# Values, memory queries and three gate sets of layer 2 as seven block products each (Strassen), in a stage of their own with the memory attention

## The chip, the cores and the metric

The kernel runs on one core of a Trainium2 chip. The metric is the device time of one execution in microseconds (us), the median of several runs. Engines are named as in the profile: PE is TensorE (PEld its weight loads), DVE is VectorE, ACT ScalarE, POOL GpSimd, and SP the engine that issues every DMA of this kernel, in order, from one queue.

## The reference

One sequence of 2048 tokens with 1024 features runs through two layers. What matters here is layer 2:

```python
def dilated_mixer(h, w_in):
    for g, (window, dil) in enumerate(((128, 1), (512, 4), (2048, 16))):
        base = g * 3 * 768
        qkv = (h @ w_in[:, base:base + 3 * 768]).reshape(B, T, 3, 6, 128)
        q, k = partial_rope(qkv[:, :, 0], pos), partial_rope(qkv[:, :, 1], pos)
        o, lse = dilated_group(q, k, qkv[:, :, 2], window, dil)
        outs.append(o); lses.append(lse)
    wts = softmax(stack(lses), axis=0)
    o = einsum('gbth,gbthd->bthd', wts, stack(outs)).reshape(B, T, 768)
    q_mem, gate = split(h @ w_in[:, 6912:], [256], axis=-1)
    return o, q_mem, gate

for i in range(2):
    h = rmsnorm(x, norm_w[i])
    mix, q_mem, gate = gla_mixer(h, ...) if i == 0 else dilated_mixer(h, w_in_b[0])
    mem_o = memory_attention(q_mem, mem_n, w_memkv[i])
    x = x + (concatenate([mix, mem_o], -1) * silu(gate)) @ w_out[i]
return rmsnorm(x, final_norm_w)
```

The input projection of layer 2 has 8192 columns: for each of three groups g (window and dilation) 768 query, 768 key and 768 value columns (6 heads of 128), then from column 6912 on 256 memory queries, and from 7168 on 1024 gate columns. The last 256 gate columns (7936) belong to the memory attention, which has 4 heads of 64 over 256 memory tokens.

## The kernel before

Every projection is done with fp16 operands that are split into a high and a low part. `mm3` (lines 174 to 177) multiplies high by high, high by low and low by high into one fp32 accumulator, so each product of 128 features costs three matmuls, and a projection runs over eight such slices of the 1024 features (`KT` = 8).

**Layer 1** runs to about 914 us. Its last loop goes over 16 blocks of 128 tokens (`NB`): `a2_out` adds the block's output to x, `a2_h2` (from line 677) normalizes it for layer 2, transposes it on PE and writes it, split, into `h2T` ([128, 2, 8, 2048]: features on partitions; high and low part; slice of the features; token). h2T stays on chip for the whole of layer 2.

**Weights.** `load_w` (line 106) fetches 1024 x 256 columns of a matrix, sums the squares of all its elements on ACT, adds the 128 partitions' sums with a matmul against a matrix of ones (`ones`, fp32; line 124), scales the weights by the result and splits them: ACT makes the high part (line 134), DVE the low one (line 135). `load_w256` uses it for layer 2. Four weight buffers (`wpb`) rotate.

**Nine units** follow, one for each pair of heads hp (0 to 2) and each group g (0 to 2). Per unit `proj_v` (line 771) makes the values of both heads for 16 token blocks: 16 x 8 x 3 = 384 matmuls with h2T as the stationary operand and 256 weight columns moving. `proj_qk` (line 791) makes one head's queries and keys: 8 x 24 = 192 matmuls of 512 columns, the rotary step on DVE and POOL (line 809), and the split. `attend` (line 818) takes the 16 query blocks of a head in 8 steps of two: scores on PE, maximum, exponential, then `split_P` (line 165), which splits the probabilities (ACT, POOL at line 169) and transposes them by a DMA (line 170, tiles `ph` to `pt`), and the product with the values. A head's output is copied (line 874) and written to DRAM (`od`, line 875), as are the row maxima and sums (`std`, line 888). The program interleaves: the attention of a head is written around the projection of the next one, and the V projection of the next unit follows.

**Gates.** When all three groups of a head pair are done, `gate_prep` (line 893) reads the maxima and sums back (tiles `nm` and `dn`, line 898), works out the weights of the three groups and writes them to DRAM (`fd`). `gate_item` (line 928) treats one head and 512 tokens: `gate_mm` does 24 matmuls of 512 columns and the SiLU; a DMA broadcasts the weights to all partitions (`fb`, line 934), three more read the outputs of the groups (`og`, lines 937 to 939); POOL (lines 940, 945) and DVE (lines 942, 948, 949, 951) combine them; the result goes to DRAM (`brd`, line 952). The pool `gk` holds one fb and one og. Eight items make a head pair. Those of hp 0 stand in unit (1, 0), those of hp 1 in the last unit, those of hp 2 in the tail.

**The tail** (about 2337 to 2550 us) goes over 16 token blocks with the memory attention: `mem_q` (line 958) projects the queries of a block with 24 matmuls of 256 columns, `mem_scores` (line 236) transposes them on PE and makes scores, softmax and `split_P`, `mem_pv` (line 265) the product with the memory values, `mem_out` (line 967) the product with its gate. The items of hp 2 and the memory gate's tiles are placed between the blocks. Then comes the output projection (from line 1065), which reads `brd` back.

**What sets the order.** The program is written in the order above, but a scheduler that simulates the engines' times (`schedule_with_timeline_sim`, line 1165) reorders the instructions of each engine, within what buffers and data allow; each engine, and SP's queue, then runs its own list strictly in order. For matmul results there are two banks `ps_mm`, one `ps_x`, two `ps_tr`, two `ps_g` and one `ps_o`.

## Time and profile before

| | us |
|---|---|
| runs of the kernel before | 2711.78, 2716.41, 2717.67 |
| median | 2716.41 |
| profiled execution, its span | 2713.5 |
| busy PE, DVE, ACT, POOL | 2603.2, 1510.0, 1128.4, 496.9 |
| layer 1, to about | 914 |
| units up to the last one's second head | 914 to 2301 |
| last attention of the units | 2301 to 2337 |
| tail with the memory attention | 2337 to 2550 |
| output projection | 2550 to 2713 |

The profiled execution has no other time of its own than its span. The profile lists for each engine how long it was busy; matmuls overlap, so that a busy PE is not one at its peak, and the distance from one matmul's start to the next says more. The clock that PE was granted is given as a share of full speed. A row of the table by stage holds one stretch of the span; a row of grouped instructions holds the source line, engine, operation, tiles written and read, shape, count, busy time and mean duration, and the idle time before them with what ended it. Rows with three durations give lowest, middle and highest in ns, and the first and last start.

### The profile page before, as it was taken

To read this page: it belongs to the slowest core of one execution; us is meant where nothing else is said; L and a number is where in the kernel's file an instruction comes from. 1 tells how busy PE (TensorE), PEld (TensorE's weight loads), DVE (VectorE), ACT (ScalarE), POOL (GpSimd) and SP (SyncE) were. 2 spreads that over 40 slices of the span, in tenths; PEclk is the share of its full clock that TensorE was granted. 3 is DMA by queue.
4 is the path that set the end of the run, shared out by engine and by line. 5 is a ranking of instruction groups with operands and counts; after the bars stand their busy time and mean duration, and the time that the engine had idled before them with its cause. 6 is when DMAs were issued, how large, how long until landed. Compare 5 with 4: busy or idle time off the path is not lost. (4 is left out here: it accounts for less than half of the span.)

```text
span 2713.5 us, 47912 instructions
## 1 busy us (share of the span) xinstructions
PE 2603.2 (96%) x19166; PEld 1937.0 (71%) x19166; DVE 1510.0 (56%) x3349; ACT 1128.4 (42%) x2621; POOL 496.9 (18%) x421
## 2 busy tenths in 40 slices
PE   7999999999999999999999998999999999788999
PEld 6889998899988845858475474756667574455687
DVE  6445443665555466373746637465555637777433
ACT  6356444543434434252425324243433434535322
POOL 0000000010101023131313314222222313443000
PEclk9999999999999999999999999999999999899999
DMA  5242113333332213130313535122322224776543
GB/s 202 84 143 74 65 57 94 119 90 96 91 96 81 91 47 86 34 90 26 87 53 100 121 86 135 38 68 73 78 62 62 72 65 128 197 172 139 158 148 114
DMA packets 377539, 259.23 MB, mean 96 GB/s; under 512 B 250674, under 2 KB 340452, under 8 KB 377316
## 3 DMA queue, kind: packets, MB, share of 16 engines
q1 hardware_dynamic: 377316, 256.17, 33.7%
q8 instruction: 150, 2.46, 0.4%
q14 instruction: 73, 0.60, 0.1%
HBM read 149.63 MB, written 60.21 MB: 77 GB/s over the span
## 5 line engine op out<-in xcount | busy, mean ns | idle before, releaser
L175 PE MATMUL ps_mm<-w,hT 128*128 128x256 f16 (+1 forms) x1408 | 387.2, 275 | 3.7 <-DVE ws L128 1.8
L176 PE MATMUL ps_mm<-w,hT 128*128 128x256 f16 (+1 forms) x1408 | 385.9, 275 | 0.0
L177 PE MATMUL ps_mm<-w,hT 128*128 128x256 f16 (+1 forms) x1408 | 385.2, 275 | 0.4 <-DVE hT L370 0.4
L175 PE MATMUL ps_mm<-h2T,w 128*128 128x512 f16 x944 | 359.2, 380 | 0.5 <-DVE qm L232 0.4
L177 PE MATMUL ps_mm<-h2T,w 128*128 128x512 f16 x944 | 358.8, 380 | 0.6 <-DVE cols L306 0.6
L176 PE MATMUL ps_mm<-h2T,w 128*128 128x512 f16 x944 | 358.9, 380 | 0.0
L809 POOL TENSOR_TENSOR sh<-sh,rope 32x512 f32<-32x512 f32 x144 | 183.2, 1272 | 629.8 <-DVE sh L808 623.3
L177 PEld LDWEIGHTS <-w 128*128 128x128 f16 x1408 | 139.1, 99 | 148.1 <-issue 3.0
L175 PEld LDWEIGHTS <-w 128*128 128x128 f16 x1408 | 138.5, 98 | 144.5 <-issue 2.4
L176 PEld LDWEIGHTS <-w 128*128 128x128 f16 x1408 | 138.5, 98 | 144.0 <-issue 2.8
L175 PE MATMUL ps_mm<-w,h2T 128*128 128x256 f16 x840 | 229.2, 273 | 0.5 <-DVE sg L301 0.5
L176 PE MATMUL ps_mm<-w,h2T 128*128 128x256 f16 x840 | 229.5, 273 | 0.0
L177 PE MATMUL ps_mm<-w,h2T 128*128 128x256 f16 x840 | 229.4, 273 | 0.0
L854 ACT ACTIVATE pm<-pm,st,cols 128x256 f32<-128x256 f32 (+1 forms) x288 | 156.2, 543 | 135.7 <-DVE st L848 134.6
L169 POOL TENSOR_TENSOR ph<-pm,ph 128x512 f16<-128x512 f32 (+2 forms) x144 | 143.5, 1001 | 291.5 <-issue 158.8
L175 PE MATMUL ps_x<-h2T,w 128*128 128x512 f16 x464 | 177.4, 382 | 0.3 <-DVE v L787 0.3
L176 PE MATMUL ps_x<-h2T,w 128*128 128x512 f16 x464 | 177.2, 382 | 0.0
L177 PE MATMUL ps_x<-h2T,w 128*128 128x512 f16 x464 | 177.1, 382 | 0.0
L169 POOL TENSOR_TENSOR stg<-mp,stg 128x512 f16<-128x512 f32 x16 | 18.5, 1159 | 833.9 <-DMA ogd<-og 457.7
L176 PEld LDWEIGHTS <-h2T 128*128 128x128 f16 x1280 | 149.4, 117 | 10.1 <-issue 2.5
L175 PEld LDWEIGHTS <-h2T 128*128 128x128 f16 x1280 | 149.5, 117 | 7.7
L176 PEld LDWEIGHTS <-hT 128*128 128x128 f16 x1408 | 138.8, 99 | 22.3 <-issue 4.1
(317 smaller groups left out, 6102.4 us busy)
## 6 DMA issues: line engine op xcount, KB each, us to landing
stg<-in_w_in_b SPq DMA_DIRECT2D x64, 512.0 KB
od<-osb SPq DMA_DIRECT2D x72, 256.0 KB
og<-od SPq DMA_DIRECT2D x72, 256.0 KB
fb<-fd SPq DMA_DIRECT2D x24, 768.0 KB
x<-in_x SPq DMA_DIRECT2D x32, 512.0 KB
hTd<-hT SPq DMA_DIRECT2D x16, 512.0 KB
hT<-hTd SPq DMA_DIRECT2D x16, 512.0 KB
x1d<-x SPq DMA_DIRECT2D x16, 512.0 KB
```

The source lines that it names most:

```text
L169: G.tensor_tensor(out=lo, in0=src, in1=hi, op=ALU.subtract)
L175: PE.matmul(o, sh, mh, start=first, stop=False)
L176: PE.matmul(o, sh, ml, start=False, stop=False)
L177: PE.matmul(o, sl, mh, start=False, stop=last)
L809: G.tensor_tensor(out=sw, in0=sw, in1=rs, op=ALU.mult)
L854: A.activation(out=p_, in_=p_, func=AF.Exp, scale=sc, bias=st[:, j:j + 1], accum_out=st[:, 16 + j:17 + j])
```

## The change

**A stage ahead of the units.** The values of all nine (hp, g), the memory queries and the gate columns 7936 (memory), 7168 (hp 0) and 7424 (hp 1) make 13 sets of 256 columns. Each set is now computed by Strassen's scheme in Winograd's form on two-by-two blocks: tokens 0 to 1023 and 1024 to 2047, features 0 to 511 and 512 to 1023, and the two halves of the 256 columns. Seven products take the place of eight. In all of them the weights are the stationary operand and 512 tokens move, so that results come with the columns on partitions.

- `sums` (lines 764 to 786) forms sums of the blocks of h2T for 256 tokens of each half: S1, S2 and S4 in new buffers, S3 in the place of h2T's second token half and first feature half. Per call these are 7 operations on DVE, 5 on POOL and 4 on ACT, of 128 x 1024 elements. It is called for 0 to 511 ahead of the first product and for 512 to 1023 behind the first step. So that S3's place can be restored, `a2_h2` now also writes that quarter of h2T to DRAM (`a21_d`, line 702), and line 955 reads it back when the stage ends.
- `load_ws` (lines 788 to 818) fetches a set's weights and forms the sums T1 to T4 on POOL, then splits them on ACT and DVE.
- `sblock` (lines 820 to 849) does the seven products for 512 tokens of each half: 7 x 4 slices x 3 = 84 matmuls of 512 columns. ACT copies two products, DVE adds five (line 835), POOL adds two (lines 844, 845). It returns r1 and r2, the results for the two token halves. A set takes two such steps.
- `out_v` (lines 851 to 873) splits r1 and r2, turns them by two DMA transposes each (line 863) and writes them to DRAM (`vd`; line 867, or 16 small writes for each result at line 872 where g = 2). Its tiles `vh` and `vo` have one buffer each. `out_gate` finishes the SiLU and writes the gates to DRAM (`sgd`); `out_q` does that with the memory queries.
- The memory attention is in the same stage, one block a step from the fifth step on.

**The units** have no V projection: `load_v` reads a head's values back. `gate_item` reads its gate from DRAM. The items of hp 0 stand in units (1, 0) and (1, 1), those of hp 1 in (2, 0) and (2, 1), four a unit. The tail has no memory attention; it has the eight gate products of hp 2 (columns 7680), into eight buffers, and then their items.

**The matrix of ones** becomes bf16, and the two partial sums of squares are added first, so that one matmul is left of two in each weight load. In layer 1 that holds too.

The core of the diff:

```diff
-    ones = tl(cp, [P, P], F32, "ones")
+    ones = tl(cp, [P, P], BF16, "ones")
...
+        rb = tl(sp, [P, 1], BF16, "rb")
+        V.tensor_tensor(out=rb, in0=rm[:, 0:1], in1=rm[:, 1:2], op=ALU.add)
+        tot = bank(cps)[:, 0:1]
+        PE.matmul(tot, ones, rb, start=True, stop=True)
...
-        for i in range(2):
-            PE.matmul(tot, ones, rm[:, i:i + 1], start=i == 0, stop=i == 1)
...
+        Ss = {n: tl(svp, [P, 2, 4, H], F16, n) for n in ("S1", "S2", "S4")}
...
+            s = f32(1, 1, V)
+            x21 = f32(1, 0, G)
+            V.tensor_tensor(out=s, in0=s, in1=x21, op=ALU.add)
+            split(s, Ss["S1"][:, 0, :, ts], Ss["S1"][:, 1, :, ts], V)
+            x11 = f32(0, 0, G)
+            V.tensor_tensor(out=s, in0=s, in1=x11, op=ALU.subtract)
+            split(s, Ss["S2"][:, 0, :, ts], Ss["S2"][:, 1, :, ts], V)
+            G.tensor_tensor(out=x21, in0=x11, in1=x21, op=ALU.subtract)
+            split(x21, quad(1, 0, 0, ts), quad(1, 0, 1, ts), G)
+            x12 = f32(0, 1, G)
+            V.tensor_tensor(out=s, in0=x12, in1=s, op=ALU.subtract)
+            split(s, Ss["S4"][:, 0, :, ts], Ss["S4"][:, 1, :, ts], V)
+        def load_ws(c0, cps):
...
+            G.tensor_tensor(out=t13, in0=rq[:, :, :, P:2 * P], in1=top, op=ALU.subtract)
+            G.tensor_tensor(out=t24[:, 0], in0=low[:, 1], in1=t13[:, 0], op=ALU.subtract)
+            G.tensor_tensor(out=t24[:, 1], in0=low[:, 0], in1=t24[:, 0], op=ALU.subtract)
+            A.activation(out=wb[:, 2, 0], in_=top[:, 0], func=AF.Copy, scale=s)
+            A.activation(out=wa[:, 0:2, 0], in_=low, func=AF.Copy, scale=s)
+            A.activation(out=wa[:, 2:4, 0], in_=t13, func=AF.Copy, scale=s)
+            A.activation(out=wb[:, 0:2, 0], in_=t24, func=AF.Copy, scale=s)
+            for src, dst in ((top[:, 0], wb[:, 2]), (low[:, 0], wa[:, 0]), (low[:, 1], wa[:, 1]),
...
+                V.scalar_tensor_tensor(out=dst[:, 1], in0=src, scalar=s, in1=dst[:, 0], op0=ALU.mult,
+                                       op1=ALU.subtract)
...
+        def sblock(w, cc, sc):
+            ts = slice(cc * 512, (cc + 1) * 512)
...
+            def product(pl, wn, an):
+                o = bank(pl)
+                for k in range(4):
+                    mm3(o, w[wn][:, 0, k], w[wn][:, 1, k], aform[an][:, k], alow[an][:, k], k == 0, k == 3)
+                return o
+            def added(out, ps, e):
+                V.scalar_tensor_tensor(out=out, in0=ps, scalar=sc, in1=e, op0=ALU.mult, op1=ALU.add)
+            r1 = tl(c4p, [P, 2, 512], F32, "c4")
+            r2 = tl(c4p, [P, 2, 512], F32, "c4")
+            u1 = tl(uv, [P, 512], F32, "uv")
+            A.activation(out=r1[:, 0], in_=product(ps_mm, "B11", "A11"), func=AF.Copy, scale=sc)
+            added(u1, product(ps_mm, "T2", "S2"), r1[:, 0])
+            A.activation(out=r2[:, 1], in_=product(ps_x, "T1", "S1"), func=AF.Copy, scale=sc)
+            added(r2[:, 0], product(ps_mm, "T3", "S3"), u1)
+            G.tensor_tensor(out=r1[:, 1], in0=u1, in1=r2[:, 1], op=ALU.add)
+            G.tensor_tensor(out=r2[:, 1], in0=r2[:, 0], in1=r2[:, 1], op=ALU.add)
+            added(r1[:, 0], product(ps_mm, "B21", "A12"), r1[:, 0])
+            added(r2[:, 0], product(ps_x, "T4", "A22"), r2[:, 0])
+            added(r1[:, 1], product(ps_mm, "B22", "S4"), r1[:, 1])
+            return r1, r2
+        def out_v(u, cc, rs):
+            g = u[1]
+            for r, c in zip(rs, (cc, cc + 2)):
+                vh = tl(svp, [P, 2, 2, 512], F16, "vh")
...
+                A.activation(out=hi, in_=src, func=AF.Copy)
+                (V if c == cc else G).tensor_tensor(out=lo, in0=src, in1=hi, op=ALU.subtract)
+                vo = tl(svp, [P, 2, 8, P], F16, "vo")
+                for i in range(2):
+                    SY.dma_start_transpose(vo[:, i], vh[:, i].rearrange("p a n -> p (a n)"))
+                for i in range(2):
+                    vv = vo[:, i].rearrange("p (a m) d -> p a m d", a=2)
+                    if g < 2:
+                        SY.dma_start(v_d[u[0], g, i][:, :, c * 4:(c + 1) * 4, :], vv)
+                    else:
+                        dv = v_d[u[0], g, i].rearrange("p a (m r) d -> p a m r d", r=4)
+                        for q in range(4):
+                            for x in range(2):
+                                SY.dma_start(dv[c * 32:(c + 1) * 32, x, :, q], vv[q * 32:(q + 1) * 32, x])
...
+        sets = [("q", None, 6912), ("g", 6, 7936)]
+        sets += [("v", (hp, g), wbase((hp, g)) + 1536) for hp in range(3) for g in range(3)]
+        sets += [("g", 0, 7168), ("g", 2, 7424)]
+        steps = [(0, 0), (1, 0), (0, 1), (1, 1)] + [(n, cc) for n in range(2, len(sets)) for cc in range(2)]
+        loaded = {0: load_ws(sets[0][2], ps_g)}
+        sums(slice(0, 256))
+        sums(slice(256, 512))
...
+        for at, (n, cc) in enumerate(steps):
+            kind, key, c0 = sets[n]
+            w, iv = loaded[n]
...
+            if at == 0:
+                sums(slice(512, 768))
+                sums(slice(768, 1024))
...
+            p_ = at - 4
+            if 0 <= p_ <= NB:
+                if p_ > 0:
+                    mem_b(p_ - 1, sd)
+                    if p_ % 4 == 0:
+                        mem_out(p_ // 4 - 1)
+                sd = mem_a(p_) if p_ < NB else None
+        for hl in range(2):
+            SY.dma_start(h2T[:, hl, 0:4, H:T], a21_d[:, hl])
...
-    def proj_v(u, wv):
...
-                        mm3(o, vblk(h2T[:, 0, k, :], g, j), vblk(h2T[:, 1, k, :], g, j),
-                            wv[:, 0, k, :], wv[:, 1, k, :], k == 0, k == KT - 1)
...
+    def load_v(u, i):
+        vt = tl(vp, [P, 2, NB, P], F16, "v")
+        SY.dma_start(vt, v_d[u[0], u[1], i])
+        return vt
...
-        sg = gate_mm(w_, c, i, ep)
+        if sg is None:
+            sg = tl(bk, [P, 512], F32, "sg")
+            SY.dma_start(sg, sg_d[h][:, cs])
...
+        if u in ((1, 0), (2, 0)):
+            gate_prep(u[0] - 1)
+        def items_of(lo):
+            if u[0] > 0 and u[1] < 2:
+                for it in range(u[1] * 4 + lo, u[1] * 4 + lo + 2):
+                    gate_item(u[0] - 1, it // 2, it % 2)
...
+    sgs = [gate_mm(gw2, it // 2, it % 2, ge, g8) for it in range(8)]
+    load_wo(0, tl(stg, WSH, F32, "stg"), wo2[0])
+    load_wo(1, tl(stg, WSH, F32, "stg"), wo2[0])
+    for it in range(8):
+        gate_item(2, it // 2, it % 2, sgs[it])
```

In program order, three places show what moves. In the names, numbers are buffer versions: `S_1488` is S1, `S_1489` S2; `c_` are the fp32 sums.

ACT at the end of layer 1, before: a weight load (L121 to L134) stands beside the last block's normalization (L154 to L148) and the two copies into h2T (L685); the first V copy (L786) follows.

```order
L121 ACTIVATE w_11055,rm_11059<-stg_11056 128x1024 x2
L126 ACTIVATE ws_11065<-ps_g_11062,cols_88 128x1
L154 ACTIVATE e_10978,ss_10979<-x_10851 128x1024
L127 ACTIVATE ws_11065<-ws_11065,cols_88 128x1
L147 ACTIVATE rs_1440_10981<-ss_10979,cols_88 128x1
L148 ACTIVATE rs_1440_10981<-rs_1440_10981 128x1
L134 ACTIVATE w_11055<-stg_11056,ws_11065 128x1024 x2
L685 ACTIVATE h2T_5069<-ps_tr_10986 128x4x128
L685 ACTIVATE h2T_5069<-ps_tr_10993 128x4x128
L786 ACTIVATE v_11097<-ps_mm_11098 128x512
```

The same place after, in the changed kernel's line numbers:

```order
L120 ACTIVATE ws_11174<-ps_g_11172,cols_88 128x1
L121 ACTIVATE ws_11174<-ws_11174,cols_88 128x1
L158 ACTIVATE e_11036,ss_11037<-x_10907 128x1024
L806 ACTIVATE w_11166<-stg_11162,ws_11174 128x512
L807 ACTIVATE w_11165<-stg_11162,ws_11174 128x2x512
L151 ACTIVATE rs_1484_11039<-ss_11037,cols_88 128x1
L152 ACTIVATE rs_1484_11039<-rs_1484_11039 128x1
L697 ACTIVATE h2T_5109<-ps_tr_11044 128x4x128
L697 ACTIVATE h2T_5109<-ps_tr_11051 128x4x128
L772 ACTIVATE S_1488_11085<-c_1500_11122 128x4x256
L772 ACTIVATE S_1488_11085<-c_1504_11142 128x4x256
L772 ACTIVATE S_1489_11086<-c_1500_11122 128x4x256
```

Behind the last block's copies stand the copies of S1 and S2, and two copies of the first weight load are now ahead of the block's normalization.

SP's queue in a value set with g = 2, which has no counterpart before; `mh` is the memory attention's.

```order
L863 DMA_TRANSPOSE vo_12634<-vh_12631 128x8x128 x2
L872 DMA vd_2_0_74_162<-vo_12634 32x4x128 x8
L872 DMA vd_2_1_75_163<-vo_12634 32x4x128 x8
L174 DMA_TRANSPOSE mpt_12741<-mh_1736_12744 128x8x128
L863 DMA_TRANSPOSE vo_12656<-vh_12653 128x8x128 x2
L872 DMA vd_2_0_74_162<-vo_12656 32x4x128 x8
L872 DMA vd_2_1_75_163<-vo_12656 32x4x128 x8
L174 DMA_TRANSPOSE mp_12964<-mh_1768_12967 128x8x128
```

Transposes and small writes of one result follow on each other, with a memory attention's transpose between the results.

SP's queue behind the last attention, before: the maxima of hp 2 are turned into weights (`fd`) between an item of hp 1 (`og`) and the memory attention's transposes (L170).

```order
L937 DMA og_25370<-od_0_50_138 128x512
L938 DMA og_25370<-od_1_51_139 128x4x128
L939 DMA og_25370<-od_2_52_140 128x16x32
L170 DMA_TRANSPOSE mp_25248<-mh_3041_25251 128x8x128
L170 DMA_TRANSPOSE mpt_25262<-mh_3044_25265 128x8x128
L952 DMA brd_72_160<-sg_25129 512x1x128
L170 DMA_TRANSPOSE mp_25315<-mh_3055_25318 128x8x128
L170 DMA_TRANSPOSE mpt_25329<-mh_3058_25332 128x8x128
L915 DMA fd_66_154<-nm_25178 16x4x32 x3
L915 DMA fd_67_155<-nm_25178 16x4x32 x3
L934 DMA fb_25368<-fd_66_154 128x1536
```

After:

```order
L1083 DMA std_61_149<-stT_25586 16x128 x2
L1091 DMA nm_25605<-std_61_149 16x3x128
L174 DMA_TRANSPOSE pt_25571<-ph_25570 128x4x128
L1091 DMA dn_25606<-std_61_149 16x3x128
L1108 DMA fd_66_154<-nm_25605 16x4x32 x3
L1068 DMA od_2_55_143<-osb_25581 128x512
L1108 DMA fd_67_155<-nm_25605 16x4x32 x3
L1129 DMA fb_25895<-fd_66_154 128x1536
L1189 DMA stg_25891<-in_w_out 128x8x256
```

The chain from the maxima to `fb` stands without transposes of the memory attention between; on PE three of the eight gate tiles of hp 2 are inside the last attention, and the other five follow its last product.

291 lines of the change are left out of this document (156 added, 135 removed).

## The prediction

> **What bounds the kernel now.** I read the page's head first: TensorE (PE) is busy for nearly the whole span, so only its work and its gaps can move the end.
>
> ```profile
> span 2713.5 us, 47912 instructions
> PE 2603.2 (96%) x19166; PEld 1937.0 (71%) x19166; DVE 1510.0 (56%) x3349; ACT 1128.4 (42%) x2621; POOL 496.9 (18%) x421
> ```
>
> Then the table by stage: end of layer 1 with the first V projection, nine units, the last attend, the tail with the memory attention, the output projection. Columns are the stretch, its length, then busy time (count) of PE, PEld, DVE, ACT, POOL, the granted clock, the DMA share.
>
> ```profile
> 500.00:923.00 423.00, 420.63 (x4005) 378.82 (x4003) 247.74 (x560) 194.46 (x419) 34.80 (x30) 1.00 0.33 94
> 923.00:2220.30 1297.30, 1275.23 (x8784) 837.33 (x8782) 721.21 (x1720) 478.47 (x1100) 336.80 (x285) 1.00 0.28 71
> 2220.30:2337.00 116.70, 104.52 (x613) 54.43 (x611) 84.91 (x176) 52.25 (x122) 43.57 (x35) 0.96 0.61 156
> 2337.00:2550.00 213.00, 176.41 (x1237) 116.46 (x1235) 149.02 (x256) 102.42 (x250) 75.52 (x50) 0.94 0.66 162
> ```
>
> PE idles 2.4 us of the first stretch, 22.1 of the units, 12.2 and 36.6 of the last two. There the clock is 0.96 and 0.94 as well: 0.04 x 116.7 + 0.06 x 213.0 = 17.4 us more. So 66 us are lost after 2220 and hardly anything ahead of it. Everywhere else the price is the matmul's start-to-start time, read from the timeline (start, duration, engine, line):
>
> ```profile
> 1023.44 0.38 PE L176 MATMUL ps_mm<-h2T,w 128*128 128x512 f16 x1
> 1023.66 0.38 PE L177 MATMUL ps_mm<-h2T,w 128*128 128x512 f16 x1
> 930.94 0.27 PE L175 MATMUL ps_mm<-w,h2T 128*128 128x256 f16 x1
> 931.05 0.27 PE L176 MATMUL ps_mm<-w,h2T 128*128 128x256 f16 x1
> ```
>
> About 0.216 us for 512 columns and 0.1095 for 256 (medians over all of each kind; these pairs show 0.22 and 0.11).
>
> **PE work removed and added.** The 256-column groups count 840 + 440 = 1280 for each of the three lines of mm3, 3840 in all: 9 x 384 for values, 384 for memory queries. All go: 3840 x 0.1095 = 420.4 us. Three gate sets go too: 3 x 8 tiles x 24 x 0.216 = 124.4.
>
> ```profile
> L175 PE MATMUL ps_mm<-w,h2T 128*128 128x256 f16 x840 | 229.2, 273 | 0.5 <-DVE sg L301 0.5
> L175 PE MATMUL ps_x<-w,h2T 128*128 128x256 f16 x440 | 120.8, 275 | 1.6 <-DVE sg L301 1.6
> ```
>
> In their place stand 13 sets x 2 column halves x 7 products x 12 matmuls of 512 columns: 2184 x 0.216 = 471.7. Balance **-73.2**. The 64 transposes of memory queries go (0.056 each): **-3.6**.
>
> A rule of the Trainium skill speaks against that price: "TensorE: Matmul & The Clock Gate", Part 2, Back-to-back issue gap, gives a sustained 131 ns at 512 columns and 81 at 128, and calls 216 the isolated gap. Estimated from that page, with some 98 at 256, the balance would be 2184 x 0.131 - 3840 x 0.098 - 576 x 0.131 = -166. This trace does not agree: its dense stream stands at 216, so the sum goes by the rows, and the rule gets no chance of its own.
>
> The `ones` product: two fp32 matmuls (in two passes) become one bf16 matmul, in 47 loads.
>
> ```profile
> L124 PEld LDWEIGHTS ps_tr<-rm,ones x152: 186/190/332, 167.8 to 2292.2; 128*128 128x128 f32 x152
> L176 PEld LDWEIGHTS <-w 128*128 128x128 f16 x1408 | 138.5, 98 | 144.0 <-issue 2.8
> ```
>
> Four loads of 190 ns become one of about 98: 47 x (0.760 - 0.098) = 31 us if nothing hides them, 0 if they fit into the 29% of the span in which PEld is free. I take **-10**, nearer to nothing, since hardly any idle time of PE shows in the units, where most of them lie. In sum PE has **-86.8** less to do.
>
> **Start of the new stage, +18 (8 to 50).** The last chain of layer 1 lay under V matmuls; now nothing of layer 2 can start without h2T of token block 15 being past ACT's queue, where the sums stand behind it.
>
> ```profile
> 905.50 0.48 DVE L671 SCALAR_TENSOR_TENSOR x<-ps_x,cj,x 128x256 f32<-128x256 f32 x1 [2.14 <-PE ps_x L177]
> 907.81 1.28 DVE L680 SCALAR_TENSOR_TENSOR sg<-x,rs,nwb 128x1024 f32<-128x1024 f32 x1
> 911.86 1.08 ACT L685 ACTIVATE h2T<-ps_tr 128x512 f16<-128x512 f32 x2 [2.01 <-PE ps_tr L162]
> L134 ACT ACTIVATE w<-stg,ws 128x1024 f16<-128x1024 f32 (+1 forms) x80 | 87.5, 1141 | 26.0 <-DVE ws L128 25.9
> L135 DVE SCALAR_TENSOR_TENSOR w<-stg,ws,w 128x1024 f16<-128x1024 f32 (+1 forms) x80 | 104.5, 1329 | 12.4 <-ACT w L134 12.0
> L169 POOL TENSOR_TENSOR mh<-mp,mh x16: 1147/1157/3662, 2351.1 to 2523.1; 128x512 f16<-128x512 f32 x16
> ```
>
> 905.5 to 912.9 is 7.4 us; 1.6 of it are PE's own transposes, so 5.8 are bare. For S1 a slice takes an ACT copy and two DVE operations (1.14 + 2 x 1.33 = 3.8), the second slice 1.3 more: 5.1. S2 needs four DVE operations (5.3) and T1*S1 covers 2.6 of them: 2.7. S3's low part is on POOL, 2 x 1.16 = 2.3 for 1024 columns: 2. Clock after the wait: 2. Sum 17.6. Lower end: all sums ahead of block 15, 5.8 + 2. Upper end: two slices wholly behind it and in series, 14 DVE operations (18.6) and 10 of POOL (23) with the 5.8 and 2. Nearer to the lower, since slices 0 and 1 need only tokens to 511 and to 1535.
>
> **Body of the stage, +15 (3 to 81).** A pass is 84 x 0.216 = 18.1 us of PE. Behind it each of two results per pass goes through one `vh` and one `vo`: copy, low part, two transposes, writes; SP serves its queue in order, so a write that waits for its transpose holds the next transposes, those of the memory attention too.
>
> ```profile
> L170 SPq DMA_TRANSPOSE pt<-ph x144: 1188/1232/3202, 999.2 to 2330.1; - x144
> 1808.64 3.33 DMA pt<-ph
> 2142.47 5.14 DMA pt<-ph
> 2366.65 4.93 DMA fb<-fd
> L875 SPq DMA_DIRECT2D od<-osb x72: 320/348/2239, 1013.0 to 2340.8; - x72
> ```
>
> One result takes transpose, landing, write landing: 1.23 + 3.33 + 3.33 = 7.9, or 1.23 + 5.14 + 4.93 = 11.3. Two are 15.8 to 22.6 against 18.1: nothing, or 4.5 x 18 value passes = 81. The lower end is the 2.4 us idle of the first stretch. With g=2 SP itself has 4 x 1.23 + 32 x 0.35 = 16.1 us a pass plus a landing per result (2 x 3.33): 22.8, or 4.7 over in 6 passes = 28, of which five c4p buffers, more than a pass, absorb about half: 15.
>
> **Hand-over to the units, +2 (0 to 8).** The restore of h2T's half moves 2 MB under the last four products, and chunks 0 and 1 of the next projection don't need it.
>
> **Units, +15 (0 to 30).** A unit loses its cover of V matmuls, 141.5 - 42.0 = 99.5 us of PE; DVE goes from 75.0 to about 66.8 (8 x 0.69 for V's low parts and 2 x 1.33 of a weight load gone), 67%. Four units get four items each, in place of one unit with eight.
>
> ```profile
> 1012.30:1153.80 141.50, 140.53 (x992) 96.48 (x990) 75.02 (x184) 50.96 (x118) 37.40 (x32) 1.00 0.27 68
> 1439.50:1653.40 213.90, 202.12 (x1262) 123.70 (x1261) 123.95 (x257) 78.83 (x166) 66.38 (x47) 0.98 0.42 107
> ```
>
> Eight items with a unit left PE idle 11.8 us: 1.5 an item; 16 make 24, and nine units some 1.4 each 13: 37 against 22.1 now.
>
> **Tail, -25 (-40 to -5).** The 66 us lost after 2220 have other work around them. The last attend ran 2301 to 2337 with five gate tiles (26 us) inside; now three are (15.6), with some 5 of its own: 15 idle. After it the chain to the first item, begun at 2340.19 with the read of the maxima:
>
> ```profile
> 2301.00:2337.00 36.00, 29.80 (x192) 17.36 (x190) 24.71 (x51) 16.14 (x43) 16.08 (x13) 0.86 0.88 216
> 2340.19 0.47 SPq L898 DMA_DIRECT2D nm<-std  x1
> L940 POOL TENSOR_TENSOR fb<-og,fb x24: 1259/1982/2103, 1399.3 to 2483.6; 128x512 f32<-128x512 f32 x24
> L945 POOL TENSOR_TENSOR fb<-og,fb x24: 1512/1532/2498, 1401.2 to 2485.6; 128x512 f32<-128x512 f32 x24
> L948 DVE TENSOR_TENSOR fb<-fb x24: 679/693/1657, 1402.8 to 2488.2; 128x512 f32<-128x512 f32 x24
> ```
>
> To fb's issue at 2366.65, then 4.93 + 1.98 + 1.53 + three DVE operations of 0.7 to 1.05: 41 us from 2337. Without memory transposes in SP's queue I take 7 off; the second item, the write and the reload add 12: 46, under which five gate tiles put 26: 20 idle. Clock 6. 15 + 20 + 6 = 41 against 66.
>
> **Sum.** -86.8 + 18 + 15 + 2 + 15 - 25 = -61.8: span 2713.5 to 2651.7; the median of the runs lies 2.9 above the span (2716.41), so **2655 us**. A change under 0.2% (5.4 us) can't be told from none.
>
> **The rivals.** *A, denser:* sums run ahead, loops fit, gate tiles cover the last chain: start 8, body 3, hand-over 0, units 3, tail -40: -112.8, **2604**. For it: the first stretch loses 2.4 us in 423. Against it: single `vh`, `vo`, `fb`.
>
> *B, POOL and DVE slow each other:* the sums (20 POOL, 28 DVE operations in one place) and the items run both at once. L940 spreads from 1259 to 2103 ns and L948 from 693 to 1657. If the start doubles (36, +18) and each of 16 items pays 0.96 more (+15): -28.8, **2688**. The Trainium skill has that mechanism in "GPSIMD Engine Reference", 1. Specifications: the two share their SBUF interfaces when VectorE has two SBUF inputs. The trace agrees in the spread alone; it doesn't show which partner causes it.
>
> *C, slower: the value outputs set the pass.* A result of 12.5 us (11.3 and one memory transpose of 1.23 in between) makes a pass 25.0, 6.9 over, 18 times 124 in place of the 15: +109, **2764**. It passes the time of before at (18.1 + 76.8 / 18) / 2 = 11.2 us a result. For it: in-order SP, one buffer. Against it: memory blocks lengthen PE's passes too, and most landings are near 3.3.
>
> *D:* gains and gaps cancel, within 5 us of 2716.
>
> **How the numbers follow.** Forecast 0.57, A 0.13, B 0.16, C 0.11, D 0.03. The range 2592 to 2714 holds the forecast with its body to 2.2 times its term and more, A with 12 us to spare, B; it leaves out C and some of the body's upper bound. Faster: forecast, A, nearly all of B, 0.85; same 0.04; slower 0.11.
>
> **What would show it.** Steps: 512-column spacing still 0.216; about 18 us idle after layer 1; a value pass of 18 to 20 us for g of 0 and 1, 20 to 23 for g=2; items at 1.5 us of PE idle; some 35 us idle around the last attend. It is wrong if value passes stand above 22 us with PE waiting for c4p (C), if POOL is the releaser at the stage's start (B), or if the tail keeps its 66 us.

## The result and the profile after

The changed kernel takes 2788.53 us (median of 4 runs, 2783.9 to 2791.84) against 2717.04 before: a ratio of 1.0268, interval [1.0253, 1.0283]. It is 71 us slower, where 61 faster were forecast. The page's head:

```profile
span 2785.2 us, 44184 instructions
PE 2553.5 (92%) x16725; PEld 1679.4 (60%) x16725; DVE 1697.5 (61%) x3514; ACT 1205.8 (43%) x2635; POOL 735.5 (26%) x550
```

PE has less to do and idles more: 231.7 us instead of 110.3. The table by stage of the changed kernel (up to 500 us; end of layer 1, sums and the first four passes; the value and gate passes; the units up to the middle of the last attend; from there to the output projection; the output projection):

```profile
0.00:500.00 500.00, 464.96 (x3783) 414.67 (x3784) 249.21 (x579) 257.99 (x625) 6.26 (x22) 0.98 0.31 106
500.00:1060.00 560.00, 505.22 (x4273) 407.63 (x4271) 363.98 (x660) 250.87 (x501) 133.66 (x74) 0.95 0.31 85
1060.00:1541.00 481.00, 437.62 (x2209) 205.60 (x2208) 251.64 (x393) 224.05 (x360) 185.88 (x118) 0.97 0.63 145
1541.00:2516.00 975.00, 924.00 (x5496) 484.33 (x5495) 708.07 (x1714) 395.67 (x982) 373.12 (x314) 0.99 0.48 125
2516.00:2581.00 65.00, 35.55 (x182) 17.50 (x181) 38.85 (x66) 31.14 (x56) 14.71 (x12) 0.74 0.54 164
2581.00:2785.20 204.20, 186.18 (x792) 149.71 (x792) 85.72 (x105) 46.09 (x113) 21.91 (x11) 0.94 0.50 165
```

And the kernel before, in the stretches that answer to them (500 to 923 stands in the prediction):

```profile
0.00:500.00 500.00, 470.39 (x3843) 422.48 (x3844) 248.16 (x565) 258.78 (x628) 6.25 (x22) 0.99 0.31 106
923.00:2301.00 1378.00, 1349.96 (x9203) 874.40 (x9201) 781.41 (x1846) 514.58 (x1178) 364.29 (x306) 1.00 0.29 74
2301.00:2550.00 249.00, 206.21 (x1426) 133.81 (x1424) 173.73 (x306) 118.56 (x292) 91.60 (x63) 0.93 0.69 170
2550.00:2713.50 163.50, 156.05 (x699) 127.53 (x697) 59.00 (x75) 42.02 (x104) 0.00 (x0) 0.99 0.38 135
```

Count a stretch's loss as PE's idle time and the busy time times the missing clock. A reader can work out each row; for 500 to 1060 it is 54.8 + 0.05 x 505.2 = 80.0.

| stretch | before | after | difference | forecast |
|---|---|---|---|---|
| to 500 us | 34.3 | 44.3 | +10 | 0 |
| end of layer 1, sums, first passes | 2.4 | 80.0 | +78 | +18 |
| value and gate passes | - | 56.5 | +56 | +15 |
| hand-over and units | 28.0 | 60.2 | +32 | +17 |
| last attend and tail | 57.2 | 38.7 | -19 | -25 |
| output projection | 9.0 | 29.2 | +20 | 0 |

The forecast of -25 counts from 2220 on, the row from 2301. The losses grew by some 178 and the span by 71.7, so PE's own work shrank by some 106 (86.8 forecast); the clock's second digit alone leaves some 13 us open in each kernel. The tail came near its forecast; the start, the passes and the units were sized too small, and the first and the last row stood at nothing.

**The start.** PE's waits in the timeline of the changed kernel (start, duration, in brackets the idle time and its releaser):

```profile
931.34 1.94 PE L166 MATMUL ps_tr<-ident,sg 128*128 128x128 f32 x8 [6.14 <-DVE sg L692]
935.85 0.61 PE L179 MATMUL ps_x<-S,w 128*128 128x512 f16 x1 [2.58 <-ACT S L772]
946.09 0.58 PE L179 MATMUL ps_mm<-S,w 128*128 128x512 f16 x1 [3.94 <-ACT S L772]
949.20 0.59 PE L180 MATMUL ps_mm<-S,w 128*128 128x512 f16 x1 [2.53 <-DVE S L773]
957.12 0.59 PE L179 MATMUL ps_mm<-h2T,w 128*128 128x512 f16 x1 [3.55 <-ACT c L840]
961.01 0.38 PE L179 MATMUL ps_x<-h2T,w 128*128 128x512 f16 x1
961.22 0.38 PE L180 MATMUL ps_x<-h2T,w 128*128 128x512 f16 x1
```

The last transposes of layer 1 wait, then each product for its sum. The last two rows show that matmuls, once they run without a break, are 0.21 to 0.22 us apart as before; the price per matmul held. Between the waits, from 937 to 959, most stood 0.43 apart, twice as far; the granted clock of 908 to 960 is 0.73. The first write of a `uv` tile in a pass marks its pace: the first stands at 959.9, the first value pass at 1062.9 (four passes, 103 us for 73 of work), the first gate pass behind the values at 1470.7: 22.66 us for each of 18 value passes in the mean, where 18.1 and about 2 of a memory block are PE's.

**The value passes.** SP's queue in a set with g = 2 of the changed kernel (start, duration of the issue, line):

```profile
1199.95 1.23 SPq L174 DMA_TRANSPOSE mpt<-mh  x1
1201.47 2.62 SPq L863 DMA_TRANSPOSE vo<-vh  x2
1204.74 9.01 SPq L872 DMA_DIRECT2D vd<-vo  x16
1213.86 0.59 SPq L899 DMA_DIRECT2D qmT<-qmd  x1
```

A result's 16 writes take SP 9.0 us of issuing (0.56 each, against 0.35 assumed), and with the transposes 14 go by until the queue is free. PE meets the stage's losses as waits for full product banks and for the memory attention's transposes:

```profile
PE ps_mm L179 <- DVE uv L835: 11.6, 3, 6.1
PE ps_o L284 <- DMA mp<-mh: 11.4, 6, 5.3
PE ps_o L284 <- DMA mpt<-mh: 5.4, 6, 1.4
PE ps_mm L179 <- DVE c L835: 5.2, 3, 4.5
```

(Waits of PE from 1060 to 1541: total, times, longest.) No single one is large: ACT, DVE, POOL and SP run in-order lists, and a late buffer in one holds the others.

The loss is uneven. From 1062.9 to 1470.7 PE idles 39 us, and 35 of them lie in these four stretches, about half of that time:

```profile
1140.90:1192.50 51.60, 41.47 (x205) 18.77 (x204) 26.73 (x45) 24.30 (x41) 19.80 (x13) 0.93 0.67 141
1234.00:1286.20 52.20, 42.47 (x238) 21.34 (x235) 30.74 (x53) 29.84 (x54) 20.62 (x14) 0.93 0.80 175
1330.80:1378.70 47.90, 39.10 (x195) 18.46 (x196) 19.18 (x33) 15.27 (x28) 18.05 (x11) 0.93 0.70 154
1421.40:1470.70 49.30, 43.23 (x210) 19.80 (x208) 22.58 (x37) 21.73 (x30) 17.30 (x11) 0.97 0.68 147
```

They are the passes in which the memory attention's output is finished, behind every fourth block (lines 911 to 917): its gate is read into a `uv` buffer and its product written from there to DRAM, both through SP's queue. The pool has two such buffers, and each pass needs one. So the memory attention shares in the passes' loss. How much is its own and how much comes from the value outputs ahead of it in the queue isn't shown: no run takes it out of the stage.

**Units and tail.** In the units PE's waits for the row maxima grew, those for transposed probabilities fell; before, then after:

```profile
PE ps_o L175 <- DMA pt<-ph: 18.6, 15, 3.3
PE ps_g L175 <- DVE mx L843: 4.9, 6, 1.3
```

```profile
PE ps_g L179 <- DVE mx L1037: 23.3, 21, 3.6
PE ps_o L179 <- DMA pt<-ph: 13.6, 19, 2.2
```

At the end one wait of 20 us stands ahead of the output projection, as long as the forecast had it; behind it the later gate items are made beside the output projection, and PE waits again for the split of the branch that is read back (the second row, from 2581 on):

```profile
2580.93 0.77 PE L179 MATMUL ps_x<-wh,w 128*128 128x512 f32 x1 [20.00 <-POOL fb L1135]
...
PE ps_mm L179 <- ACT w L1216: 9.4, 2, 6.3
```

### The profile page after: what moved, and what is told of

Its sections match the earlier page's. It is cut to its first block, busy times and chain, and to the rows that moved or that the text cites. A ratio compares the mean times of both kernels' runs of the same rounds, so it can differ in the third digit from the quotient of the medians.

```text
span 2785.2 us, 44184 instructions
## 1 busy us (share of the span) xinstructions
PE 2553.5 (92%) x16725; PEld 1679.4 (60%) x16725; DVE 1697.5 (61%) x3514; ACT 1205.8 (43%) x2635; POOL 735.5 (26%) x550
## 5 line engine op out<-in xcount | busy, mean ns | idle before, releaser
L179 PE MATMUL ps_mm<-h2T,w 128*128 128x512 f16 x1128 | 435.5, 386 | 29.3 <-ACT c L840 12.7
L181 PE MATMUL ps_mm<-h2T,w 128*128 128x512 f16 x1128 | 435.2, 386 | 0.0
L180 PE MATMUL ps_mm<-h2T,w 128*128 128x512 f16 x1128 | 435.1, 386 | 0.0
L180 PEld LDWEIGHTS <-w 128*128 128x128 f16 x1944 | 192.3, 99 | 251.3 <-issue 55.0
L181 PEld LDWEIGHTS <-w 128*128 128x128 f16 x1944 | 192.6, 99 | 223.8 <-issue 21.3
L179 PEld LDWEIGHTS <-w 128*128 128x128 f16 x1944 | 192.7, 99 | 221.9 <-issue 16.6
L179 PE MATMUL ps_x<-h2T,w 128*128 128x512 f16 x504 | 192.2, 381 | 0.4 <-ACT c L842 0.4
L181 PE MATMUL ps_x<-h2T,w 128*128 128x512 f16 x504 | 192.5, 382 | 0.0
L180 PE MATMUL ps_x<-h2T,w 128*128 128x512 f16 x504 | 192.4, 382 | 0.0
L179 PEld LDWEIGHTS <-hT 128*128 128x128 f16 x1408 | 139.1, 99 | 24.4 <-issue 5.4
L180 PEld LDWEIGHTS <-hT 128*128 128x128 f16 x1408 | 139.0, 99 | 23.7 <-issue 5.3
L181 PEld LDWEIGHTS <-hT 128*128 128x128 f16 x1408 | 139.5, 99 | 18.2 <-DVE hT L382 0.7
L114 ACT ACTIVATE w<-stg 128x1024 bf16<-128x1024 f32 (+1 forms) x78 | 82.0, 1051 | 113.5 <-DMA stg<-in_w_in_b 70.2
L859 ACT ACTIVATE vh<-c 128x1024 f16<-128x1024 f32 x36 | 60.4, 1678 | 131.7 <-DMA vo<-vh 78.5
L179 PE MATMUL ps_g<-k,q 128*128 128x256 f16 (+1 forms) x288 | 70.2, 251 | 31.0 <-DVE mx L1037 26.6
```

The source lines that it names most:

```text
L114: A.activation(out=junk[i], in_=hv, func=AF.Square, accum_out=rm[:, i:i + 1])
L179: PE.matmul(o, sh, mh, start=first, stop=False)
L180: PE.matmul(o, sh, ml, start=False, stop=False)
L181: PE.matmul(o, sl, mh, start=False, stop=last)
L859: A.activation(out=hi, in_=src, func=AF.Copy)
```

## The experiments

My theory after the result had three parts: the sums and the bare end of layer 1 set the start; the value outputs through SP's queue set the passes (rival C); lost cover sets the units. The rival for the first two was B, that DVE and POOL slow each other. All ratios are to the kernel before on the same chip; the changed kernel is 1.0268, and 0.1% is 2.7 us. e1, e5, e6, e7 and e9 leave out part of the work; they measure what it costs and are no versions to use.

| run | ratio | interval |
|---|---|---|
| e1_no_sums | 1.0127 | [1.0112, 1.0142] |
| e2_sums_dve | 1.0239 | [1.0224, 1.0254] |
| e3_stage_dve | 1.0183 | [1.0166, 1.0200] |
| e4_g2_merge | 1.0226 | [1.0211, 1.0241] |
| e5_no_sums_blocks | 1.0056 | [1.0037, 1.0075] |
| e6_two_vh_vo | 1.0147 | [1.0132, 1.0163] |
| e7_before_v_eighth | 0.9034 | [0.9018, 0.9051] |
| e8_vo2 | 1.0348 | [1.0331, 1.0365] |
| e9_no_out_transposes | 0.9927 | [0.9911, 0.9944] |
| e10_two_sets_direct | 1.0238 | [1.0222, 1.0253] |
| e11_combined | 1.0044 | [1.0029, 1.0060] |
| e12_tail_two_fb | 1.0265 | [1.0249, 1.0280] |
| e13_before_ones | 1.0049 | [1.0035, 1.0063] |
| e14_four_sets_direct | 1.0154 | [1.0138, 1.0170] |
| e15_writes_on_pool | 1.0163 | [1.0148, 1.0177] |
| e16_three_sets_direct | 1.0097 | [1.0083, 1.0112] |
| e17_combined_fp32_ones | 1.0077 | [1.0063, 1.0091] |
| e18_changed_fp32_ones | 1.0228 | [1.0214, 1.0242] |

### The sums: e1, e5, e2

In both, `sums` does nothing. e1:

```diff
+        for n in Ss:
+            G.memset(Ss[n], 0.0)
...
+            return
```

> The sums over h2T are left out: S1, S2, S4 are zeros set early, S3's block of h2T stays as it is (so the values are wrong); all products, outputs and units are unchanged. In the changed kernel PE loses some 87 us to idle time and clock from 500 us to the fourth product pass, against 2.4 before. If the sums cause that, the time falls from 2788 to about 2705 to 2720 and layer 1 ends at 914 to 918 again. If it is the bare chain of the last block of layer 1, as I had priced the start, 18 us stay and some 30 go: about 2755.

e5, with blocks of h2T for S1, S2 and S4:

```diff
-        Ss = {n: tl(svp, [P, 2, 4, H], F16, n) for n in ("S1", "S2", "S4")}
+        Ss = {"S1": (1, 1), "S2": (0, 0), "S4": (0, 1)}
...
-                aform[n], alow[n] = Ss[n][:, 0, :, ts], Ss[n][:, 1, :, ts]
+                aform[n], alow[n] = quad(*Ss[n], 0, ts), quad(*Ss[n], 1, ts)
```

> As e1_no_sums, but the products that read S1, S2 and S4 read blocks of h2T itself (values wrong), so that there is no memset for PE to wait for, and 48 KB a partition are free. Compared with e1 the 7 us wait for POOL's memset goes, some more at half clock: about 2735; a value pass stays at 22.6 us.

e1 gave 38 us back, e5 57 (2.12% of 2712). e1 lies between its two expectations; PE waited 7.0 us there for POOL's memset of S1. e5 has no memset and came out 7 us below its expectation. In e5 the first `uv` stands at 927.8 and the first value pass at 1001.9: 61 of the 78 us of the start are the sums. The rest, 17, is the end of layer 1 without its cover (counted as above, e5 loses 16 from 500 to 1002). A pass stayed at 22.5.

e2 puts POOL's operations of the sums and weight loads on DVE:

```diff
-            x21 = f32(1, 0, G)
+            x21 = f32(1, 0, V)
...
-            G.tensor_tensor(out=t13, in0=rq[:, :, :, P:2 * P], in1=top, op=ALU.subtract)
+            V.tensor_tensor(out=t13, in0=rq[:, :, :, P:2 * P], in1=top, op=ALU.subtract)
```

> Every POOL operation in the sums and in the weight loads of the stage goes to DVE; the work is the same. Ports theory (DVE and POOL stretch each other when both run): DVE's 128x1024 operations fall from 2 to 3 us back to 1.2 to 1.3, the start loses 45 instead of 87: about 2745. Work theory (the start is the mere number of operations, the body is set by the output loop): DVE has 12 operations a slice in place of 7, 15 us in place of 9, the start gets longer by about 10: about 2795.

The groups of the sums' operations, changed kernel first (lowest, middle and highest in ns), then e2:

```profile
L773 DVE TENSOR_TENSOR S<-c,S x12: 1212/1944/3361, 934.9 to 1006.1; 128x1024 f16<-128x1024 f32 x12
L768 POOL TENSOR_TENSOR c<-h2T x12: 2119/2899/3147, 893.7 to 989.2; 128x1024 f32<-128x1024 f16 x12
```

```profile
L773 DVE TENSOR_TENSOR S<-c,S x12: 1206/1218/1226, 927.2 to 993.0; 128x1024 f16<-128x1024 f32 x12
L768 DVE TENSOR_TENSOR c<-h2T x16: 1206/1216/1695, 892.7 to 977.4; 128x1024 f32<-128x1024 f16 x16
```

Rival B's mechanism is there: beside POOL a DVE operation takes 1.94 us in the middle and up to 3.36; alone (e2) it takes 1.22. That is the contention that the Trainium skill names in "GPSIMD Engine Reference", 1. Specifications, and here the runs agree. What e2 gains is small: the first value pass came 17.6 us earlier, the whole 8 us, since DVE then has 48 sum operations, some 58 us. Both expectations missed. Taking POOL out of the stage's start removes the contention and adds work to DVE, and the two nearly cancel; the price of the contention by itself isn't shown.

### The value passes: e3, e4, e6, e8, e9

e3 is e2, and POOL's additions and low parts of the products go to DVE too:

```diff
-            G.tensor_tensor(out=r1[:, 1], in0=u1, in1=r2[:, 1], op=ALU.add)
...
+            V.tensor_tensor(out=r1[:, 1], in0=u1, in1=r2[:, 1], op=ALU.add)
...
-                (V if c == cc else G).tensor_tensor(out=lo, in0=src, in1=hi, op=ALU.subtract)
+                V.tensor_tensor(out=lo, in0=src, in1=hi, op=ALU.subtract)
```

> As the one before, and the two adds of a pass and the low part of the second result go from POOL to DVE too, so POOL does nothing in the products' stage but the memory attention's split. Ports theory: a value pass falls from 22.7 us to about 21, 18 times 1.7 = 30 less than the one before, about 2715. Output-loop theory: a pass stays at 22.7, within 8 of the one before.

15 us less than e2; a pass went from 22.89 in e2 to 22.14. That is half of what the ports theory wanted, and more than the 8 of the output-loop theory.

e4 halves the number of small writes:

```diff
-                            for x in range(2):
-                                SY.dma_start(dv[c * 32:(c + 1) * 32, x, :, q], vv[q * 32:(q + 1) * 32, x])
+                            SY.dma_start(dv[c * 32:(c + 1) * 32, :, :, q], vv[q * 32:(q + 1) * 32])
```

> The 16 small writes of a result with g = 2 become 8 of twice the size; nothing else changes. Output-loop theory (SP's queue and one vo buffer set the pass): 8 issues of 0.43 us or more go from each of 12 results, 3.4 us each, 41 in all, of which the buffers ahead had hidden a part: 2750 to 2765. Ports theory: within 5 of 2788.

11 us less than the changed kernel, a pass at 21.64. The gain is smaller than both bounds expected (23 to 38), since a write of twice the size takes SP 609 ns in place of 430:

```profile
L871 SPq DMA_DIRECT2D vd<-vo x96: 550/609/1675, 1169.6 to 1470.8; - x96
```

```profile
L872 SPq DMA_DIRECT2D vd<-vo x192: 302/430/1805, 1166.7 to 1491.5; - x192
```

The second fence is the changed kernel.

e6 is e5 with two buffers for vh and vo, e8 the changed kernel with two for vo and four c4p:

```diff
+        vop = cv.enter_context(pool("vop", 2))
...
-                vh = tl(svp, [P, 2, 2, 512], F16, "vh")
+                vh = tl(vop, [P, 2, 2, 512], F16, "vh")
...
-                vo = tl(svp, [P, 2, 8, P], F16, "vo")
+                vo = tl(vop, [P, 2, 8, P], F16, "vo")
```

> As e5, and vh and vo have two buffers each. Output-loop theory: with both buffers the serial chain copy, low part, transposes, writes no longer sets the pass; it falls from 22.6 us to PE's own 18.1 + 2 = 20.1, 18 times 2.5: 45 less than e5. Queue theory (SP's time itself, 16 writes of 0.43 us a result with g = 2): passes of g < 2 go to 20.1, those of g = 2 stay near 23.8: 22 less than e5. Ports theory: nothing, within 5 of e5.

```diff
-        c4p = cv.enter_context(pool("c4p", 5))
+        c4p = cv.enter_context(pool("c4p", 4))
...
+        vop = cv.enter_context(pool("vop", 2))
...
-                vo = tl(svp, [P, 2, 8, P], F16, "vo")
+                vo = tl(vop, [P, 2, 8, P], F16, "vo")
```

> The changed kernel with two vo buffers, paid for by one of the five c4p buffers. Output-loop theory: the next result's transposes no longer wait for this one's writes; a pass falls from 22.7 to about 21: 25 to 30 less, about 2755. If instead the products need five c4p buffers, PE waits for c4p and it gets slower than 2785. Ports theory: within 5.

e6 missed on the other side: it is 25 us slower than e5 (a pass 23.8). e8 is 22 slower than the changed kernel, which its expectation had for the case that the products need five c4p buffers. What SP's transposes wait for in the value passes (total, times, longest), e5 and then e6:

```profile
SPq L852 <- DMA vd<-vo: 31.9, 21, 4.5
...
SPq L852 <- DVE vh L849: 6.8, 4, 3.0
...
SPq L852 <- DVE mden L288: 3.9, 1, 3.9
```

```profile
SPq L853 <- DVE vh L850: 35.5, 7, 9.5
SPq L853 <- DVE mden L288: 30.4, 4, 10.8
```

In e6 these transposes wait for DVE's low part and behind DVE's work for the memory attention, and no longer for SP's own writes. With more buffers the scheduler puts transposes further ahead in an in-order queue, and there they hold everything behind them. That this order is the cause is argued from the waits, not shown by a run. In e8 the first value pass already starts 12 us later (1075.1), before any value output has run, so more than half of its loss isn't the output's; the lost c4p buffer is the likely reason. Its passes take 23.0.

e9 is e5 with a value result written as it stands, without transposes, `vo` and small writes:

```diff
-                vo = tl(svp, [P, 2, 8, P], F16, "vo")
                 for i in range(2):
-                    SY.dma_start_transpose(vo[:, i], vh[:, i].rearrange("p a n -> p (a n)"))
...
+                    SY.dma_start(v_d[u[0], g, i][:, :, c * 4:(c + 1) * 4, :],
+                                 vh[:, i].rearrange("p a (m d) -> p a m d", d=P))
```

> As e5_no_sums_blocks, and a value result's vh goes to DRAM by two writes, without the two transposes, without vo and without the small writes (values wrong). Output-loop theory (transposes, vo and SP's time set the pass): a pass falls from 22.5 us to 20.2, 41 less than e5. Engine-queue theory (the copies, low parts and adds that wait for each other in the in-order lists of ACT, DVE and POOL set it): a pass stays above 21.5, less than 18 off.

35 us less than e5, and a pass at 20.60: close to the output-loop theory's 41 and 20.2. The value passes of e5, then of e9:

```profile
1005.00:1407.00 402.00, 364.25 (x1892) 173.61 (x1891) 218.93 (x344) 188.65 (x323) 169.22 (x109) 0.97 0.66 148
```

```profile
1001.00:1372.00 371.00, 356.87 (x1899) 173.49 (x1899) 222.12 (x351) 191.03 (x327) 172.10 (x111) 0.99 0.45 122
```

Idle PE falls from 37.8 to 14.1 us, with DVE, ACT and POOL as busy as before. So most of the passes' loss goes when the transposes and what follows them on SP go; the copies and adds don't make it. Whether the one buffer, SP's time or the wait of the memory attention's transfers behind them does, e9 can't tell, since it takes all three away.

### Cover and tail: e7, e12

e7 is the kernel before with one of the eight slices in the V projection:

```diff
-                    for k in range(KT):
+                    for k in range(1):
                         mm3(o, vblk(h2T[:, 0, k, :], g, j), vblk(h2T[:, 1, k, :], g, j),
```

> The kernel before, its V projection with one of the eight feature slices (values wrong): 9 x 336 matmuls of 256 columns less, 331 us of PE. Everything else of a unit stays, so this is the lost cover alone. As I had priced it (a unit's other work has room enough, 67% of DVE): 2711 - 331 = 2380, up to 2385. Cover theory: V matmuls filled PE's waits for maxima and transposes, 25 to 40 us come back: 2405 to 2420.

2451.78 us: 331 us of matmuls go and 260 us of time, so 71 us came back as waiting, more than the cover theory's 25 to 40. Within this kernel the units and the V stretches look like this (e7):

```profile
923.00:2040.00 1117.00, 1054.68 (x6300) 574.36 (x6299) 779.31 (x1850) 509.39 (x1181) 362.79 (x307) 0.98 0.35 92
```

62 us idle, where the same stretch of the kernel before had 28; with the clock it is 83 against 28, and 10 more come at the end of layer 1. But this isn't the cover of the softmax chains alone. PE's waits for maxima and transposed probabilities grew by 2 us only (25.6 against 23.5), while 13.4 are waits for the low parts of the values (`v`, line 787), which e7 still makes, and 12 for those of queries and keys. In the changed kernel the waits for maxima grew by 18. That V matmuls covered those is argued, not shown.

e12 gives the last gate items two `fb` buffers:

```diff
-        fb = tl(gk, [P, 3, 16, 32], F32, "fb")
+        fb = tl(pl or gk, [P, 3, 16, 32], F32, "fb")
```

> The changed kernel with two fb buffers for the last eight gate items. Behind the last attention PE loses 77 us to idle time and clock, 20 of it in one wait for the first items. Item theory (fb's reload, 12 to 17 us an item, sets the tail): 15 to 30 less, 2755 to 2770. Chain theory (maxima, weights, first two items and the output weights set it, and four chunks of output projection cover the later items): within 6 of 2785.

No change (0.8 us), so the chain theory: a wait of 19.6 us stays ahead of the output projection, now put down to the split of the reloaded branch:

```profile
PE ps_x L179 <- ACT w L1216: 20.7, 2, 19.6
```

### Cover for the start, and the sum of the mends: e10, e11, e14, e15, e16

e10 makes the first two sets as direct products around the sums, and S3 in a pass of its own, which forms two of the fp32 sums a second time:

```diff
+        def direct(c):
+            out_q(c, dblock(loaded[0][0], c, SQ))
+            out_gate(6, c, dblock(loaded[1][0], c, loaded[1][1]))
...
+        direct(0)
         sums(slice(0, 256))
         sums(slice(256, 512))
...
+        direct(1)
...
+        for c in range(4):
+            sum3(slice(c * 256, (c + 1) * 256))
```

> The changed kernel, in which the first two sets (memory queries, memory gate) are direct products, 24 matmuls a tile, ahead of the first Strassen set, and S3 is made in a pass of its own behind them. PE has 2 x 5.2 = 10.4 us more to do and 83 us that need no sum. Start theory (PE has nothing to do while the last block of layer 1 and the sums run, 76 us and 18 ahead of them): 65 to 85 go, 10 come: 2705 to 2730. If the sums merely move to where PE waits for them again: within 15 of 2785.

8 us less: the second expectation. e11 below is this kernel with the edits of e3, e4 and e12. PE is busy through layer 1's end now, but from 1000 to 1040 it waits again, with DVE busy 35 of the 40 us and POOL 32:

```profile
1000.00:1040.00 40.00, 20.81 (x115) 10.55 (x113) 35.43 (x39) 21.61 (x45) 32.26 (x15) 0.71 0.25 63
```

> e10's order, with the edits of e3 (no POOL in the sums and products), of e4 (half the small writes) and two fb buffers in the tail. If they add up as measured one by one (e3 24 less, e4 11 less than the changed kernel): 2670 to 2695, below the kernel before at 2712. If the output loop takes up what the start gives, 2700 to 2720.

61 us less than the changed kernel, 2 us above the worse of its two expectations; e3, e4, e10 and e12 add up to 43 (23, 11, 8 and 1), and why together they give more is open. It is still 0.44% slower than the kernel before. In the same 40 us PE is busy 20, with DVE full (39).

e14 takes all four sets that aren't values as direct products, e16 three, both with e11's other edits; e15 is e14 with the values' writes on POOL's queue.

```diff
-        sets = [("q", None, 6912), ("g", 6, 7936)]
+        sets = [("q", None, 6912), ("g", 6, 7936), ("g", 0, 7168), ("g", 2, 7424)]
...
-        sets += [("g", 0, 7168), ("g", 2, 7424)]
```

> e11_combined with all three gate sets and the memory queries as direct products ahead of the nine value sets, so 166 us of PE need no sum: PE has 10.4 us more to do than in e11. Start theory: e11's PE still loses some 43 us to idle time and clock from 905 to 1060, where the sums fill DVE; with twice the cover about 10 are left: 2722 - 33 + 10 = 2699, below the kernel before at 2711. If the sums are late by the queue's order and not for want of time: 2725 to 2740.

```diff
-                        SY.dma_start(v_d[u[0], g, i][:, :, c * 4:(c + 1) * 4, :], vv)
+                        G.dma_start(v_d[u[0], g, i][:, :, c * 4:(c + 1) * 4, :], vv)
```

> e14 with the writes of the values to DRAM issued by POOL, which has next to nothing to do there, in place of SP. Output-loop theory: SP's queue no longer waits for a transpose to land ahead of a write; a value pass falls from about 21 us to 20.2: 10 to 15 less than e14. Against it: POOL's part of the memory attention's split stands behind those waits: as slow as e14 or up to 20 slower.

```diff
-        sets = [("q", None, 6912), ("g", 6, 7936)]
+        sets = [("q", None, 6912), ("g", 6, 7936), ("g", 0, 7168)]
...
-        sets += [("g", 0, 7168), ("g", 2, 7424)]
...
+        sets += [("g", 2, 7424)]
```

> e11_combined with one gate set (hp 0) as a third direct set, its last two chunks over the making of S3, the sums written as early as in e11, and one gate set still last in the stage. PE has 5.2 us more to do. In e11 PE is idle 24 us from 960 to 1040, with the clock at 0.71 in the second half, while DVE is busy 74 of the 80. Start theory (the sums fill DVE for some 110 us and PE lacks that much other work): 20 to 30 go, 5 come: 2695 to 2708, at or below the kernel before. Order theory (what the scheduler makes of the lists moves the time as much as the cover does, as in e14): 2715 to 2740.

All three are slower than e11, against my start theory: e14 by 30 us, above both of its expectations, e16 by 14, within what the order theory had. In e14 DVE was busy only 50 of the 110 us from 930 to 1040 and was full behind it, and the stage ended on a value set, behind which the first projection waited 16.1 us:

```profile
1040.00:1100.00 60.00, 53.61 (x271) 25.21 (x271) 57.53 (x71) 41.31 (x65) 7.06 (x4) 0.94 0.28 78
```

```profile
PE ps_x L179 <- DVE q L1049: 16.1, 1, 16.1
```

In e16 PE's longest wait near the stage's end, 12.7 us, is for `uv` again. That more cover would help if the sums stood earlier in DVE's list is argued; I didn't find an order that does it. e15 equals e14: which queue issues the writes makes no difference there. But a value pass stood at 20.3 us in e14 already, near PE's own work, so there was little to gain. No version that does the whole work beat the kernel before.

### The matrix of ones: e13, e18, e17

e13 makes this edit in the kernel before; e18 undoes it in the changed kernel and e17 in e11:

```diff
-    ones = tl(cp, [P, P], F32, "ones")
+    ones = tl(cp, [P, P], BF16, "ones")
-        for i in range(2):
-            PE.matmul(tot, ones, rm[:, i:i + 1], start=i == 0, stop=i == 1)
+        V.tensor_tensor(out=rb, in0=rm[:, 0:1], in1=rm[:, 1:2], op=ALU.add)
+        PE.matmul(tot, ones, rb, start=True, stop=True)
```

> The kernel before with the matrix of ones in bf16 and one matmul a load (the sum of the two partial sums on DVE); nothing else. My forecast's term: -10, 2701 against 2711. The upper bound (no load of the fp32 ones is hidden): -31, 2680. All hidden: 0. The losses of both traces summed, PE does some 108 us less in the changed kernel and not 86.8, which speaks for -31.

> The changed kernel with the matrix of ones in fp32 again, nothing else: that part undone. As in e13 turned round: 5 to 15 less than 2785. By PE's work: 0 to 10 more. The forecast had it at 10 more.

> e11_combined with the matrix of ones in fp32 again, two matmuls a load, no add on DVE. If the bf16 ones costs time as in e13 (13 us in the kernel before), 5 to 15 go: about 2710. By PE's work alone it should be up to 9 slower: 2722 to 2731.

An edit that takes work from PE, and gives DVE one small addition a load, made the kernel before 13 us slower; no expectation had that. PE is 9 us less busy (2594.3 against 2603.2) and waits more; DVE comes to h2T's last low parts 10 us later (before, then e13):

```profile
912.49 1.29 DVE L686 TENSOR_TENSOR h2T<-ps_tr,h2T 128x512 f16<-128x512 f32 x2 [0.94 <-ACT h2T L685]
```

```profile
922.26 0.69 DVE L687 TENSOR_TENSOR h2T<-ps_tr,h2T 128x512 f16<-128x512 f32 x1 [4.35 <-ACT h2T L686]
```

Undone in the changed kernel it gives 11 us back; undone in e11 it costs 9. So this edit is worth between +13 and -9 us. That the order which the scheduler makes around it decides is argued. Another cause isn't ruled out: the addition (`rb`) now stands in each load's chain, and at the end of layer 1 of the changed kernel PE waited 6.8 us for one of them. No run has the bf16 matrix without the addition. The work saved ahead of 500 us came back as waiting: PE is busy 464.0 us there in e13 against 470.4, and the loss as counted above is 45 against 34, as in the changed kernel.

## Why the prediction was wrong

**PE's work** held: 216 ns a matmul, and some 106 us less against the 86.8 forecast, with 13 open in each kernel. The 131 ns that the Trainium skill gives ("TensorE: Matmul & The Clock Gate", Part 2, Back-to-back issue gap) show in neither trace.

**"Start of the new stage, +18"** is the largest miss: 78 measured, beyond its own upper end of 50. The step that failed priced the wait of the first products for two slices and let the rest lie beside products. In fact four slices, 28 DVE and 20 POOL operations, came between 893 and 1008 with two weight loads, and the first four passes took 103 us for 73. A low part of a sum took DVE 1.94 us there (the middle of line 773), not 1.33. The sums made 61 of the 78 (e5). The end of layer 1 without cover, priced at 5.8 + 2 of clock, made 17.

**"Body of the stage, +15"** was sized too small: 56, within its bounds of 3 to 81. That the value outputs in SP's queue lengthen the pass is borne out by e9. A pass took 22.66 us for two results: 11.3 each, close to the break-even that rival C named (11.2). SP's writes with g = 2 took 0.43 to 0.56 us and not 0.35. What the step put no price on is the memory attention's own use of that queue and of the two `uv` buffers: 35 of the 39 us that PE idles stand in the passes where its outputs are finished. Those eight passes took 25.1 us each in the mean, the other ten 20.7. That two buffers don't mend it (e6, e8) was not foreseen.

**"Units, +15"** with the hand-over's 2: 32. The price of 1.4 us idle a unit took DVE's 67% for room enough. The waits for DVE's row maxima grew from 4.9 to 23.3 us, so it wasn't. What holds DVE there, the lost cover or the gate items in four units, no run separates.

**"Tail, -25"** held up to the output projection: 39 us lost where the sum had 41, and the wait ahead of it is 20.0 where the sum had 20. What failed is what the sum put at nothing: the gate items that now stand beside the output projection. It loses 29 us there instead of 9.

**The ones**, -10: no sign can be given to it, as e13, e18 and e17 show.

**Rivals.** C came true in its side and in part of its mechanism, at 22.66 us a pass and not 25.0; its sign, PE waiting for c4p, shows only in part, since the longest waits are for `uv` and the memory attention's transposes. Its 2764 lacked the start. B is real in the durations, but taking POOL's work away gave 8 us (e2), 23 with that of the products (e3). A was wrong. I gave 0.11 to the only case on this side, though the body's upper end and the start's upper end together already passed zero: 32 + 66 = 98 against a gain of 61.8. The bounds stood in the text and were not added.

## What to carry to other kernels

Work that leaves a full engine can uncover waits that it hid. Before a change that saves matmuls, sum what the new stage asks of every in-order list in the stretch where it all arrives at once, and add the upper bounds of the terms together, since they fall due together. One small edit, meant to save 10 us, cost 13 in one kernel and 11 in another and gave 9 in a third, so where a scheduler sets the order a small gain counts only when timed in its place. And a mean over passes hides where the loss lies: look at the passes one by one before naming what sets them.
